# Loading the dense U columns by whole blocks into three buffers

## The chip, the cores and the metric

One core of a Trainium2 chip runs the whole kernel in one launch. The metric is device time in microseconds, the median of repeated runs. TensorE multiplies, VectorE and ScalarE split and copy, GpSimd issues row gathers, SyncE (SP) issues the plain loads. Each engine works through its own queue in order.

## The reference, cut to what matters

One residual block over T = 256 tokens of width D = 2048. Its last part is a retrieval layer over 16,384 = 128 x 128 experts. For every token and each of 8 heads the scores of two halves of a key choose 16 experts; with `emb_u` and `emb_v` (16,384 x 2048, f32):

```
u = emb_u[it];  a = einsum('td,thkd->thk', xt, u)
w = gelu(a) * gate
vv = emb_v[it]; y = einsum('thk,thkd->td', w, vv)
```

So for each token 128 rows of `emb_u` are dotted with the token's vector, and 128 rows of `emb_v` are summed with the weights that result.

## The kernel before

**The U stage.** The dots with `emb_u` are done in two ways at once. The first 768 of the 2048 columns (`UG`) are gathered: GpSimd fetches, for one of the 128 choices and 128 tokens, 128 rows of 768 columns (L757), and VectorE multiplies and sums them (L764). The other 1280 columns (`FK` = 10 slices of 128) are dense: all 16,384 experts are multiplied with all tokens on TensorE, and the wanted numbers are picked out later, from a table `A`. The dense part runs over 128 blocks of 128 experts, a block in two halves of 5 slices each: 256 half blocks, `n` = 0 to 255.

**One half block.** `u_load` (L702) loads 128 x 5 x 128 f32 (320 KB, 2560 contiguous bytes to a partition) into one of `UB` = 4 buffers `ub`. For n >= `DIRECT` = 34 it splits them so that TensorE can take them in its faster f32r format: ScalarE casts to `hi` (L711), VectorE subtracts, `lo = ub - hi` (L712), each into one of `UHB` = 3 buffers. `u_products` (L887) then makes 5 slices x 3 products: hi by both parts of the tokens' vectors, lo by the first. The half blocks below 34 are multiplied as they are, in f32 (`mmu<-x1T,ub`), straight out of `ub`. Four half blocks, two blocks of experts, share a PSUM bank; ScalarE copies it into `A` (L954).

**Order around it.** The first `FIRST` = 3 loads are issued before the routing jobs (L742). The room of `A` is free only when those jobs' tiles are, so the first finished bank is parked in a tile `set` (L907), which takes a buffer of the `ulo` tag, and is copied into `A` once the split operands 34 and 35 have been made (L956). 64 gathers are made early, during the routing; 16 are left for the stage after. The others are spread over the products at 0.733 a half block from n = 16 on: each waits for the products of its half block (L962), and its dot is put behind the lo split that was made last (L945), at most two gathers lying in flight before it (`BEHIND_U`). Gathers take four buffers: free `hT` tiles and one row tile.

The queues' orders are not written out by hand: a planner puts each instruction into its engine's queue by the time at which it expects the operands, so a load can stand before another that the program issues first. A buffer's load waits for the last reader of what lay there.

**After it.** The picking stage turns one-hot rows by a product with an identity in f32r, `idr`, which is cast on ScalarE in `columns()` (L873, called at n = `COLS`, but placed earlier by the planner). Then the V stage does the same with `emb_v`: dense columns as blocks of 736 KB (5888 contiguous bytes to a partition), split likewise, and gathered rows of 576 columns.

Of the kernel before, what the change touches and what calls it, by code (L numbers as in the profile page):

```python
# [10 lines left out]
F32 = mybir.dt.float32  # L11
F32R = mybir.dt.float32r
# [4 lines left out]
ALU = mybir.AluOpType  # L17
# [5 lines left out]
P = 128  # L23
T = 256
# [23 lines left out]
SC, QH = 3, 2  # L48
FIRST, DIRECT = 3, 34
EG, LG = 7, 2  # L50
UB, UHB = 4, 3
PRE, POOL, LEFT = 16, 0, 16
ADA_FROM, ADA_EVERY = 0, 3.4
LEAD, LAG, AHEAD1 = 1, 2, 1
# [6 lines left out]
FK = KD - UK  # L61
# [55 lines left out]
def block_kernel(ctx, tc, a, out):  # L117
    nc = tc.nc
    def pool(name, side, bufs=1, space=None):
        stack = ExitStack()  # L120
        kw = {} if space == bass.MemoryType.DRAM else {"reuse_waits": "tile"}
        if space is not None:
            kw["space"] = space
        return stack.enter_context(tc.tile_pool(name=name, bufs=bufs, side=side, **kw)), stack
# [5 lines left out]
    late = {}  # L130
# [9 lines left out]
    def bank(name):  # L140
        return late["side"].tile([P, 512], F32, tag="side", name=name)
# [5 lines left out]
    ident = kst[:, K_ID:K_ID + P]  # L147
# [159 lines left out]
    for j in range(D // GC + 1):  # L307
# [12 lines left out]
        if old is not None:  # L320
            hi, lo = loaded.pop(old)
# [376 lines left out]
    u_rows, u_cols, v_rows, v_cols = a["peer_u_rows"], a["peer_u_cols"], a["peer_v_rows"], a["peer_v_cols"]  # L698
    HALF = ((0, FK - FK // 2), (FK - FK // 2, FK))
    UH = FK - FK // 2  # L700

    def u_load(n):  # L702
        ub = late["p2"].tile([P, UH, P], F32, tag="ub", bufs=UB, name="ub")
        k0, k1 = HALF[n % 2]
        w = k1 - k0
        nc.sync.dma_start(ub[:, :w], u_cols[n // 2, :, k0:k1])
        if n < DIRECT:
            return ub, ub
        hi = late["p2"].tile([P, UH, P], F32R, tag="uhi", bufs=UHB, name="uhi")
        lo = late["p2"].tile([P, UH, P], F32R, tag="ulo", bufs=UHB, name="ulo")  # L710
        late["hi"] = nc.scalar.copy(hi[:, :w], ub[:, :w])  # L711
        late["lo"] = (nc.gpsimd if n < POOL else nc.vector).tensor_tensor(lo[:, :w], ub[:, :w], hi[:, :w].bitcast(F32), op=ALU.subtract)  # L712
        return hi, lo

    def norm2():
        drain()
        nc.sync.dma_start(ga2d, adaR[96:97])
        ssum = late["ssum"] = keep.tile([P, TT], F32, name="ssum")
        nc.vector.tensor_reduce(ssum, late["ss"], axis=AX.X, op=ALU.add)
        rsqrt(ssum, ssum, 1.0 / D)  # L720
        pr = bank("prs")
        for tt in range(TT):
            nc.tensor.matmul(pr[:, tt * P:(tt + 1) * P], ssum[:, tt:tt + 1].to_broadcast([P, P]), ident, start=True, stop=True)
        for c in range(KD // 2):
            v = late["x1T"][:, 2 * c:2 * c + 2]
            nc.vector.tensor_tensor(v, v, pr[:, None, :T].to_broadcast([P, 2, T]), op=ALU.mult)
            dst = h2T.add("h2T")
            for k in range(2):
                nc.scalar.activation(v[:, k], v[:, k], AF.Identity, bias=shc[:, 2 * c + k:2 * c + k + 1])
            put_split(dst, slice(0, 2), v)  # L730
        for c0 in range(0, UG, GC):
            psh = ada_bcast(1, c0, "psh2")
            for tt in range(TT):
                hr = h2b[:, tt, c0:c0 + GC]
                nc.vector.scalar_tensor_tensor(hr, hr, ssum[:, tt:tt + 1], psh, op0=ALU.mult, op1=ALU.add)
        sb_s.close()
        pg, late["pg_s"] = pool("pg", "left")
        late["pg"] = pg
        late["p2"], late["p2_s"] = pool("p2", "right")
        late["skT"] = pg.tile([P, 2 * HEADS, NK], F32, name="skT")  # L740
        nc.sync.dma_start(late["skT"], a["peer_subkeys"])
        late["u"] = [u_load(n) for n in range(FIRST)]  # L742
        late["pair"] = pg.tile([P, TT * 2, TOPK], F32, name="pair")
        nc.sync.dma_start(late["pair"].rearrange("p s a -> p (s a)"), a["const_index"][:, K_PAIR:])
# [125 lines left out]
        nc.vector.tensor_tensor(ex, ex, sm[:, :, :, None].to_broadcast([P, TT, HEADS, TOPK]), op=ALU.mult)  # L870

    def columns():
        nc.scalar.copy(idr, ident)  # L873
        for dst, src in ((i1T, i12[:, 0]), (i2T, i12[:, 1]), (gT, gate)):
            pt = bank("pt")
            for tt in range(TT):
                nc.tensor.transpose(pt[:, tt * P:(tt + 1) * P], src[:, tt], ident)
            nc.scalar.copy(dst, pt[:, :T])
            if dst is i2T:
                nc.scalar.mul(neg, pt[:, :T], -1.0)  # L880

    p2, p2_s = late["p2"], late["p2_s"]
# [4 lines left out]
    def u_products(n):  # L887
        for m in range(n + len(ready), min(n + (3 if n < DIRECT else 2), 2 * NK)):
            ready.append(u_load(m))
        hi, lo = ready.pop(0)  # L890
        first, last = n % 2 == 0, n % 2 == 1
        if n % 4 == 0:
            sums[n // 4] = bank("mmu").rearrange("p (b t) -> p b t", b=2) if n // 4 % 2 else pm.tile([P, 2, T], F32, tag="mm", name="mmu")
        acc = sums[n // 4][:, n // 2 % 2]
        k0, k1 = HALF[n % 2]
        steps = ((hi, 0), (hi, 1), (lo, 0)) if n >= DIRECT else ((hi, None),)
        for i, (w, part) in enumerate(steps):
            for k in range(k0, k1):
                x = late["x1T"][:, UK + k] if part is None else h2T.op(part, UK + k)
                mm = nc.tensor.matmul(acc, w[:, k - k0], x, start=(first and k == 0 and i == 0),  # L900
                                      stop=(last and k == FK - 1 and i == len(steps) - 1))
        return mm
# [1 line left out]
    staged = {}  # L904

    def stage(g):
        t = p2.tile([P, 2, T], F32, tag="ulo", bufs=UHB, name="set")  # L907
        nc.scalar.copy(t, sums.pop(g))
        staged[g] = t

    for n in range(DIRECT):
        mm = u_products(n)
        if n % 4 == 3 and not staged:
            stage(n // 4)
# [11 lines left out]
    pick_room, pick_room_s = pool("pickroom", "left")  # L926
    colT = pick_room.tile([P, 4, T], F32, name="colT")
    i1T, i2T, wT, gT = (colT[:, i] for i in range(4))
    neg = pick_room.tile([P, T], F32, name="neg")
    idr = pick_room.tile([P, P], F32R, name="idr")  # L930
    row_room, row_room_s = pool("rowroom", "left")
    flown, begun = [], 0

# [15 lines left out]
    for n in range(2 * NK):  # L949
        if n >= DIRECT:  # L950
            mm = u_products(n)
        if n % 4 == 3:
            src = staged.pop(n // 4) if n // 4 in staged else sums.pop(n // 4)
            put = nc.scalar.copy(A[:, n // 4], src.rearrange("p b (g s) -> p g b s", s=2))  # L954
            if n < DIRECT:
                tc.add_manual_dep(put.ins, split_ahead.ins.name, QUEUED, reason="the first split operands before the table")  # L956
        if n == COLS - 12:
            softmax(mm)
        if n == COLS:
            columns()  # L960
        while done < rate * (n + 1 - PRE):
            fly_u(*todo.pop(0), after=mm)  # L962
            done += 1
        while len(flown) > BEHIND_U:
            land_u()
# [10 lines left out]
    p2, p2_s = pool("pm2", "right")  # L976
# [4 lines left out]
        return b, b.rearrange("p (t n) -> p t n", t=4)  # L981

    agT = p2.tile([P, T], F32, name="agT")
    SET = 8
    iotas = iota[:, None, :].to_broadcast([P, SET, P])
    o1s, o2s = {}, {}

    def one_hot(q, u, on):
        t0 = u * SET
        o = p2.tile([P, SET, P], F32R if q else F32, tag=f"o{q}", bufs=O2 if q else O1, name="oh")  # L990
        ii = colT[:, q]
        cut = SET - (SHARE1 if u * SET < T // 2 else SHARE2)[q]
        if on == "V":
            nc.vector.tensor_tensor(o[:, :cut], iotas[:, :cut], ii[:, t0:t0 + cut, None].to_broadcast([P, cut, P]), op=ALU.is_equal)
        else:
            for t in range(cut):
                nc.scalar.activation(o[:, t], iota, AF.Square, bias=neg[:, t0 + t:t0 + t + 1])
            nc.scalar.activation(o[:, :cut], o[:, :cut].bitcast(F32), AF.Relu, bias=1.0, scale=-1.0)
        for t in range(cut, SET):
            nc.gpsimd.tensor_scalar(o[:, t], iota, ii[:, t0 + t:t0 + t + 1], None, op0=ALU.is_equal)  # L1000
        return o
# [3 lines left out]
    def turned(u):  # L1005
        for h in range(2):
            t0 = u * SET + 4 * h
            oh = p2.tile([P, 4, P], F32, tag="oh2T", bufs=OT, name="oh2T")
# [256 lines left out]
```

## Time and profile before

| | |
|---|---|
| median of 3 runs | 2291.24 us (2289.45 to 2292.52) |
| the profiled execution | 2295.83 us, its span 2294.0 us |
| TensorE busy | 2144.0 us, 93% |
| VectorE busy | 1784.8 us, 78% |
| ScalarE busy | 994.7 us, 43% |
| GpSimd busy | 941.0 us, 41% |
| DMA | 638.25 MB, mean 278 GB/s |
| granted TensorE clock, mean | 0.984 of full speed |

The span runs from the first to the last instruction of the profiled execution. Busy shares are averages over stages that have different limits. A row of the grouped view names line, engine, operation, output<-input, shape and count, then busy time and mean length, then the idle time of that engine just before these instructions and what ended it. PE is TensorE, PEld its weight loads, DVE is VectorE, ACT ScalarE, POOL GpSimd, SPq the queue of SP.

### The profile page before, as it was taken

The page shows a single profiled execution, that of the slowest core. Times are in us where ns is not written, and L with a number is a line of the kernel's source. Part 1 is how long each engine was busy: PE and PEld are TensorE (multiplying, and loading weights), DVE is VectorE, ACT ScalarE, POOL GpSimd, SP SyncE. Part 2 cuts the span into 40 slices and gives each one's busy share as a digit, 9 for nine tenths or more (in the row PEclk, how much of TensorE's full clock was granted, in tenths as well). Part 3 has the DMA queues.
Part 4 walks back from the last instruction along what each step waited for, and adds up shares of the span by engine and source line. Part 5 has one row for each costly group of instructions (what it writes and reads, how often), then busy time and mean ns, then how long its engine had stood idle before and what let it go on. Part 6 is the DMA issues. An engine that isn't in the chain of part 4 may idle for free. (4 is left out here: it accounts for less than half of the span.)

```text
span 2294.0 us, 37061 instructions
## 1 busy us (share of the span) xinstructions
PE 2144.0 (93%) x13886; PEld 1915.3 (83%) x13886; DVE 1784.8 (78%) x3400; ACT 994.7 (43%) x1424; POOL 941.0 (41%) x748
## 2 busy tenths in 40 slices
PE   6899999999999998999599999997889999999996
PEld 3578888999999977988589999997788887888885
DVE  3469888888888855688677777778997888888887
ACT  3235556553344445100244444446775434444443
POOL 0000000000000001566644444447996878878884
PEclk9999999999999999999899999998999999999998
DMA  9987787788878866668889999994205999999997
GB/s 356 371 308 267 285 284 278 276 291 291 298 281 292 310 212 216 220 221 282 284 303 324 324 317 314 306 325 138 62 2 179 335 325 327 327 337 328 334 328 269
DMA packets 144311, 638.25 MB, mean 278 GB/s; under 512 B 20721, under 2 KB 26625, under 8 KB 112001
## 3 DMA queue, kind: packets, MB, share of 16 engines
q1 hardware_dynamic: 102146, 459.65, 56.4%
q0 software_dynamic: 41984, 176.23, 22.6%
q8 instruction: 109, 1.79, 0.3%
q14 instruction: 72, 0.59, 0.1%
HBM read 631.59 MB, written 4.20 MB: 277 GB/s over the span
## 5 line engine op out<-in xcount | busy, mean ns | idle before, releaser
L757 POOL DMA_INDIRECT gat<-in_peer_v_rows,eidx x256 | 414.3, 1619 | 105.7 <-issue 40.9
L757 POOL DMA_INDIRECT gat<-in_peer_u_rows,eidx x256 | 316.0, 1234 | 284.9 <-PE mmu L900 190.4
L213 ACT CAST whi<-wt 128x2048 fp32r<-128x2048 f32 x128 | 244.4, 1909 | 274.7 <-PE mm L414 208.7
L764 DVE SCALAR_TENSOR_TENSOR gat<-gat,h2b 128x768 f32<-128x768 f32 x256 | 250.3, 980 | 117.4 <-DMA gat<-in_peer_u_rows,eidx 110.4
L215 DVE TENSOR_TENSOR wlo<-wt,whi 128x2048 fp32r<-128x2048 f32 (+1 forms) x128 | 289.3, 2260 | 53.0 <-ACT whi L213 49.4
L358 POOL DMA_DIRECT2D br<-in_b_ada x32 | 15.8, 495 | 763.8 <-DVE ada_acc L359 718.3
L900 PE MATMUL mmu<-h2T,uhi 128*128 128x256 f32 x2220 | 307.6, 286 | 11.4 <-ACT uhi L711 11.2
L1126 ACT CAST vh<-vb 128x1472 fp32r<-128x1472 f32 x128 | 183.1, 1430 | 299.2 <-DMA vb<-in_peer_v_cols 242.8
L711 ACT CAST uhi<-ub 128x640 fp32r<-128x640 f32 x222 | 161.3, 728 | 319.5 <-DMA ub<-in_peer_u_cols 265.7
L900 PEld LDWEIGHTS mmu<-h2T,uhi 128*128 128x128 f32 x2220 | 283.9, 193 | 17.0 <-ACT uhi L711 16.8
L1109 DVE SCALAR_TENSOR_TENSOR yg<-gat,wrow,yg 128x576 f32<-128x576 f32 x254 | 207.7, 818 | 73.2 <-DMA gat<-in_peer_v_rows,eidx 68.9
L355 DVE SCALAR_TENSOR_TENSOR ada_acc<-wa,sc_col,ada_acc 128x256 f32<-128x256 f32 x480 | 231.8, 483 | 11.5
L1128 DVE TENSOR_TENSOR vl<-vb,vh 128x1472 fp32r<-128x1472 f32 x128 | 215.7, 1685 | 12.6 <-ACT vh L1126 12.4
L1178 PE MATMUL yp<-vl,wh 128*128 128x512 f32 (+1 forms) x768 | 194.8, 387 | 11.5 <-DVE vl L1128 10.5
L900 PE MATMUL mmu<-h2T,ulo 128*128 128x256 f32 x1110 | 174.3, 288 | 32.8 <-DVE ulo L712 30.8
L1178 PE MATMUL yp<-vh,wh 128*128 128x512 f32 (+1 forms) x768 | 193.1, 385 | 4.5 <-ACT wh L1122 2.3
L712 DVE TENSOR_TENSOR ulo<-ub,uhi 128x640 fp32r<-128x640 f32 x222 | 180.1, 823 | 16.3 <-ACT uhi L711 12.4
L1178 PE MATMUL yp<-vh,wl 128*128 128x512 f32 (+1 forms) x768 | 192.1, 384 | 0.0
L900 PEld LDWEIGHTS mmu<-h2T,ulo 128*128 128x128 f32 x1110 | 150.1, 193 | 39.1 <-DVE ulo L712 34.9
L414 PE MATMUL mm<-whi,hT 128*128 128x512 f32 (+1 forms) x832 | 181.8, 363 | 0.0
L1178 PEld LDWEIGHTS yp<-vl,wh 128*128 128x128 f32 x768 | 142.1, 188 | 46.7 <-DVE vl L1128 20.6
L1178 PEld LDWEIGHTS yp<-vh,wh 128*128 128x128 f32 x768 | 144.9, 189 | 31.1 <-ACT vh L1126 3.5
(276 smaller groups left out, 3650.1 us busy)
## 6 DMA issues: line engine op xcount, KB each, us to landing
wa<-in_w_ada SPq DMA_DIRECT2D x96, 1024.0 KB
vb<-in_peer_v_cols SPq DMA_DIRECT2D x128, 736.0 KB
ub<-in_peer_u_cols SPq DMA_DIRECT2D x256, 320.0 KB
wt<-in_w_vg SPq DMA_DIRECT2D x32, 1024.0 KB
wt<-in_w_branch_gate SPq DMA_DIRECT2D x32, 1024.0 KB
wt<-in_w_u SPq DMA_DIRECT2D x16, 1024.0 KB
wt<-in_w_b_out SPq DMA_DIRECT2D x16, 1024.0 KB
wt<-in_w_o SPq DMA_DIRECT2D x16, 1024.0 KB
```

The lines of the kernel that those rows point to most:

```text
L213: nc.scalar.copy(hi, wt)
L215: nc.vector.tensor_tensor(lo[:, :cut], wt[:, :cut], hi[:, :cut].bitcast(F32), op=ALU.subtract)
L355: nc.vector.scalar_tensor_tensor(acc, wt[:, k], s, acc, op0=ALU.mult, op1=ALU.add)
L414: nc.tensor.matmul(job.ps[b], l, r, start=(first and k == 0 and i == 0 and not lo_part), stop=(last and k == job.rows - 1 and lo_part == 1))
L712: late["lo"] = (nc.gpsimd if n < POOL else nc.vector).tensor_tensor(lo[:, :w], ub[:, :w], hi[:, :w].bitcast(F32), op=ALU.subtract)
L757: d = nc.gpsimd.indirect_dma_start(out=g, out_offset=None, in_=table, in_offset=bass.IndirectOffsetOnAxis(ap=rows_of("idx")[:, tt, n:n + 1 ...
L764: return nc.vector.scalar_tensor_tensor(g, g, 1.0, h2b[:, tt, :UG], op0=ALU.mult, op1=ALU.mult, accum_out=pe["wrow"][:, tt, n:n + 1])
L900: mm = nc.tensor.matmul(acc, w[:, k - k0], x, start=(first and k == 0 and i == 0), stop=(last and k == FK - 1 and i == len(steps) - 1))
L1109: d = nc.vector.scalar_tensor_tensor(yg[:, tt], g, w, yg[:, tt], op0=ALU.mult, op1=ALU.add)
L1126: nc.scalar.copy(vh, vb)
L1128: late["split"] = nc.vector.tensor_tensor(vl, vb, vh.bitcast(F32), op=ALU.subtract)
L1178: return nc.tensor.matmul(yp[tt][n][:, :w], l[:, tt * P:(tt + 1) * P], r[:, c:c + w], start=(i == 0 and j == 0), stop=(i == NK - 1 and j = ...
```

## The change

Dense columns are loaded once a block (n even), all ten slices, 640 KB, 5120 contiguous bytes to a partition, into one of three buffers; the two halves are views of it. The split still goes by halves, into three hi buffers and two lo buffers in place of three. The parked bank takes a buffer of the hi tag. The f32r identity moves from the room that lasts through the U stage to that of the picking stage, and its cast from `columns()` to where that room is opened. In bytes of a partition: `ub` 10,240 to 15,360, lo 7680 to 5120.

```diff
-UB, UHB = 4, 3
+UB, UHB, ULB = 3, 3, 2
...
     def u_load(n):
-        ub = late["p2"].tile([P, UH, P], F32, tag="ub", bufs=UB, name="ub")
         k0, k1 = HALF[n % 2]
         w = k1 - k0
-        nc.sync.dma_start(ub[:, :w], u_cols[n // 2, :, k0:k1])
+        if n % 2 == 0:
+            late["ub"] = late["p2"].tile([P, FK, P], F32, tag="ub", bufs=UB, name="ub")
+            nc.sync.dma_start(late["ub"], u_cols[n // 2])
+        ub = late["ub"][:, k0:k1]
         if n < DIRECT:
             return ub, ub
         hi = late["p2"].tile([P, UH, P], F32R, tag="uhi", bufs=UHB, name="uhi")
-        lo = late["p2"].tile([P, UH, P], F32R, tag="ulo", bufs=UHB, name="ulo")
-        late["hi"] = nc.scalar.copy(hi[:, :w], ub[:, :w])
-        late["lo"] = (nc.gpsimd if n < POOL else nc.vector).tensor_tensor(lo[:, :w], ub[:, :w], hi[:, :w].bitcast(F32), op=ALU.subtract)
+        lo = late["p2"].tile([P, UH, P], F32R, tag="ulo", bufs=ULB, name="ulo")
+        late["hi"] = nc.scalar.copy(hi[:, :w], ub)
+        late["lo"] = nc.vector.tensor_tensor(lo[:, :w], ub, hi[:, :w].bitcast(F32), op=ALU.subtract)
         return hi, lo
...
     def columns():
-        nc.scalar.copy(idr, ident)
...
     def stage(g):
-        t = p2.tile([P, 2, T], F32, tag="ulo", bufs=UHB, name="set")
+        t = p2.tile([P, 2, T], F32, tag="uhi", bufs=UHB, name="set")
...
-    idr = pick_room.tile([P, P], F32R, name="idr")
...
     agT = p2.tile([P, T], F32, name="agT")
+    idr = p2.tile([P, P], F32R, name="idr")
+    nc.scalar.copy(idr, ident)
```

## Rows read from the trace of the kernel before

**Rows 1.** The page: busy us and instructions; DMA share and GB/s in 40 slices.

```profile
PE 2144.0 (93%) x13886; PEld 1915.3 (83%) x13886; DVE 1784.8 (78%) x3400; ACT 994.7 (43%) x1424; POOL 941.0 (41%) x748
...
DMA  9987787788878866668889999994205999999997
GB/s 356 371 308 267 285 284 278 276 291 291 298 281 292 310 212 216 220 221 282 284 303 324 324 317 314 306 325 138 62 2 179 335 325 327 327 337 328 334 328 269
```

**Rows 2.** Windows, U stage: length; busy us (count) by engine; clock, DMA share, GB/s.

```profile
1110.00:1150.00 40.00, 25.57 (x162) 23.86 (x163) 26.53 (x51) 13.68 (x23) 23.70 (x19) 0.84 0.87 285
1150.00:1550.00 400.00, 382.04 (x3083) 372.37 (x3082) 300.71 (x512) 173.87 (x262) 176.69 (x151) 1.00 0.94 317
```

**Rows 3.** Timeline of TensorE, 1096 to 1121: start, length, what, [idle before <-releaser].

```profile
1096.89 1.45 PE L900 MATMUL mmu<-h2T,uhi 128*128 128x256 f32 x10
1110.60 1.43 PE L900 MATMUL mmu<-h2T,ulo 128*128 128x256 f32 x5 [12.26 <-DVE ulo L712]
...
1116.59 1.47 PE L900 MATMUL mmu<-h2T,uhi 128*128 128x256 f32 x10 [1.36 <-ACT uhi L711]
```

**Rows 4.** Grouped instructions of 1150 to 1550 us.

```profile
L900 PE MATMUL mmu<-h2T,uhi 128*128 128x256 f32 x2052 | 282.1, 284 | 7.8 <-ACT uhi L711 7.8
L900 PEld LDWEIGHTS mmu<-h2T,uhi 128*128 128x128 f32 x2051 | 260.1, 191 | 12.4 <-ACT uhi L711 12.2
...
L712 DVE TENSOR_TENSOR ulo<-ub,uhi 128x640 fp32r<-128x640 f32 x206 | 167.1, 823 | 11.9 <-ACT uhi L711 8.3 <-PE mmu L900 1.4 <-issue 0.8
L900 PE MATMUL mmu<-h2T,ulo 128*128 128x256 f32 x1025 | 159.1, 286 | 10.1 <-DVE ulo L712 8.1 <-issue 1.3
L711 ACT CAST uhi<-ub 128x640 fp32r<-128x640 f32 x205 | 148.9, 728 | 227.9 <-DMA ub<-in_peer_u_cols 181.2 <-PE mmu L900 32.4 <-DVE ulo L712 9.3
...
L900 PEld LDWEIGHTS mmu<-h2T,ulo 128*128 128x128 f32 x1025 | 137.2, 191 | 15.2 <-DVE ulo L712 11.0 <-issue 4.0
```

**Rows 5.** Timeline of TensorE in the steady part, 1305 to 1316 us.

```profile
1307.45 0.76 PE L900 MATMUL mmu<-h2T,ulo 128*128 128x256 f32 x5
1308.05 1.36 PE L900 MATMUL mmu<-h2T,uhi 128*128 128x256 f32 x10
1309.25 0.76 PE L900 MATMUL mmu<-h2T,ulo 128*128 128x256 f32 x5
1309.85 1.36 PE L900 MATMUL mmu<-h2T,uhi 128*128 128x256 f32 x10
```

**Rows 6.** Waits, 1150 to 1550: us in total, times, longest.

```profile
DVE gat L764 <- DMA gat<-in_peer_u_rows,eidx: 84.8, 89, 4.0
```

**Rows 7.** Windows, the V stage.

```profile
1800.00:2250.00 450.00, 438.80 (x1961) 365.27 (x1960) 382.73 (x443) 190.69 (x217) 366.85 (x224) 1.00 0.94 330
```

**Rows 8.** Timeline of SP's queue, 1098 to 1112 us.

```profile
1110.57 1.76 SPq L706 DMA_DIRECT2D ub<-in_peer_u_cols  x4
```

**Rows 9.** Line 706 up to 1093.5: ns min/median/max, first and last start.

```profile
L706 SPq DMA_DIRECT2D ub<-in_peer_u_cols x36: 327/328/913, 904.7 to 1092.8; - x36
```

**Rows 10.** Waits of SP's queue, 1090 to 1125, then 1150 to 1550.

```profile
SPq L706 <- DVE ulo L712: 21.0, 4, 14.4
...
SPq L706 <- DVE ulo L712: 230.0, 164, 3.8
```

**Rows 11.** Timeline of ScalarE, then of VectorE, 1108 to 1122 us.

```profile
1110.59 3.51 ACT L954 COPY A<-mmu 128x512 f32<-128x512 f32 x7
1115.81 0.72 ACT L711 CAST uhi<-ub 128x640 fp32r<-128x640 f32 x1 [1.71 <-DMA ub<-in_peer_u_cols]
...
1116.57 0.83 DVE L712 TENSOR_TENSOR ulo<-ub,uhi 128x640 fp32r<-128x640 f32 x1 [3.53 <-ACT uhi L711]
```

**Rows 12.** Timeline of VectorE, 1305 to 1312 us.

```profile
1307.77 0.82 DVE L712 TENSOR_TENSOR ulo<-ub,uhi 128x640 fp32r<-128x640 f32 x1
...
1309.62 1.65 DVE L712 TENSOR_TENSOR ulo<-ub,uhi 128x640 fp32r<-128x640 f32 x2
```

**Rows 13.** Line 873, the identity's cast.

```profile
L873 ACT CAST idr<-kst x1: 302/302/302, 1032.1 to 1032.1; 128x128 fp32r<-128x128 f32 x1
```

## The prediction

> **What bounds the kernel now.** I read the page first [rows 1]: TensorE is busy 93% of the span, and the DMA engines stand at 9 tenths in the slices from 1204 to 1548 us, most of the U stage, which the change is about. No view of the whole span says which of the two binds there, so the stage was cut by time [rows 2].
>
> The U stage runs with split operands from 1097 us on, in three parts: a stop of 12.3 us [rows 3], a slow ramp from 1110 to 1150 with the granted clock at 0.84 of full speed, and 400 us of steady work with the clock at 1.00 (2.4 GHz), the DMA engines at 0.94 and 317 GB/s. In the steady part TensorE makes 2052 hi and 1025 lo matmuls [rows 4], 15 to a half block, so 205 half blocks at 1.95 us. Where nothing is waited for, a half block takes 1.80 us: first products at 1308.05 and at 1309.85 [rows 5]. So 205 x 1.80 = 369 us is TensorE's floor, and 31 us is all that any change to loads and buffers can win there.
>
> Who is late? By the grouped rows of this stretch [rows 4] TensorE stands idle 7.8 us before the hi products, for ScalarE, and 10.1 us before the lo products, 8.1 of it for VectorE; seen from the weight loads that go ahead of the products it is 12.4 and 15.2, nearly the whole 31. ScalarE in turn waits 181 us for dense columns to land; VectorE is busy 300.7 us and waits another 84.8 us, 89 times, for the row gathers [rows 2, 6]. So two streams are late about equally: dense columns by way of ScalarE, gathered rows by way of VectorE, both from the same DMA engines. TensorE is nearly full and so are they.
>
> **The change part by part.**
>
> *Whole blocks, three buffers.* Four buffers of half a block become three of a whole one: six halves of room for four. Now a half's buffer is refilled as soon as its own lo split is done, and used again four halves on (4 x 1.95 = 7.8 us, of which cast, 0.73, and split, 0.82, take their part). Afterwards the first half of a block is asked for when the split five halves before it ends, the second six: 9.8 and 11.7 us, while the larger load takes 655,360 B / 317 GB/s = 2.07 us of the engines where the smaller takes 1.03. So about 1 us more per load against 2 to 4 us more time. ScalarE's waits should mostly go, and with them TensorE's 7.8 us. What is late next is VectorE, whose gathers the change does not touch.
>
> Does the DMA side allow it? The stretch moves 317 GB/s x 400 us = 126.8 MB. The contiguous piece of one partition goes from 2560 B to 5120 B for the dense half of that traffic. The nearest stretch with larger pieces of both kinds (5888 B dense, gathers beside it) is the V stage, 330 GB/s at the same share 0.94 [rows 7]. At 330 the bytes take 384 us, 16 less; at 317, nothing is won. I take the middle, 8 us, which is also TensorE's wait for ScalarE. **Term: -8 us, bounds -31** (the floor) **and +23** (late gathers, the last rival below).
>
> The Trainium skill, "DMA: Bandwidth & Descriptors", Bandwidth, counts about 2 us fixed for each transfer on top of its bytes, and wants 1 MiB transfers. An estimate from that page's fit, 2.75 us for 320 KB and 3.5 us for 640 KB, would by itself bring the loads of the steady part from 564 to 359 us if they ran one at a time, and with that the whole 31 us. The trace doesn't bear the condition out: SP issues four of these loads within 1.76 us [rows 8], so whatever is fixed in them overlaps. Its result is the time of the first rival below.
>
> *The stop and the ramp.* In the 12.3 us stop TensorE waits for the first lo split [rows 3], which VectorE comes to only behind its dots with early gathered rows; the change touches neither, 0. But the ramp has a piece of its own: SP has issued 36 half loads by 1092.8 [rows 9] and then waits 14.4 us for a lo split [rows 10], though the room of halves 36 and 37 is that of 32 and 33, which TensorE reads directly and has left at 1096.89 [rows 3]. A load that waits for a split must stand before them in SP's order. They go out from 1110.57 on [rows 8], so ScalarE waits 1.71 us, VectorE 3.53 [rows 11] and TensorE 1.36 [rows 3]. With whole blocks the room for halves 36 and 37 is that of 30 and 31, free two direct halves sooner; that load should go before the stop and be there when ScalarE's copies end at 1114.1 [rows 11]. TensorE's wait makes 1.4 us, VectorE's 3.5 pulls the rest of the ramp in, part of which the gathers take back. **Term: -3 us.** Bounds: 0 if SP's order is as unlucky again; -13 if only VectorE's 26.5 us of work stayed of the ramp's 40 [rows 2].
>
> *Two lo buffers.* A lo split then waits for the product two halves before it, not three. It hardly ever would: the split at 1307.77 and the one at 1309.62 start with products before them long over, the second of them the one of 1307.45 [rows 5, 12]. Cover is lost only when VectorE would be over two halves ahead, and it finishes the split of 1307.77 at 1308.59, 0.66 us before its product at 1309.25. **Term: 0**, bounds 0 and +8.1, TensorE's waits on VectorE doubled. The staging copy moves from a lo to a hi buffer: freed by the first of ScalarE's table copies, which stand before the third cast in any case [rows 11]; 0, and at worst 0.73, a cast's length.
>
> *Half as many issues on SP.* 128 fewer at 0.33 us [rows 9] is 42 us of SP's queue, but in the steady part SP waits 230 us for splits [rows 10]: 0. Ahead of the stage three blocks go out in place of four halves: 0, at worst the 2.07 us that the two halves more take at 317 GB/s.
>
> *The identity copy.* One ScalarE cast of 302 ns at 1032 [rows 13] moves behind the U stage, because its room is freed only there, and holds up the first one-hots by its length. **Term: +0.3 us**, bounds 0 and 1.25: a gather still in its room costs 84.8 / 89 = 0.95 us on average.
>
> Sum: -8 - 3 + 0.3 = -10.7 us. The profiled execution took 2295.83 us (span 2294.0), which is 4.6 above the median of the runs; it would take 2285.1, and the median goes from 2291.24 to **2280.5 us**.
>
> **The rivals.**
>
> *The dense loads were all of it: faster by much.* If VectorE's lateness is itself a consequence of late casts, TensorE's floor is nearly reached: -26 of the 31 us and -5 of the ramp, 2260 us. For it: ScalarE's 181 us of waiting are by far the longest on a computing engine. Against: by its own rows VectorE waits only 8.3 us for casts, and 84.8 for gathers [rows 4, 6].
>
> *Nothing moves.* The DMA engines at 0.94 are full for the purpose, the size of the pieces changes little, and each byte earlier for a cast is a byte later for a gather; or SP's order holds the new loads as it held the old. -1, 2290 us. For it: 317 and 330 GB/s differ by 4% only.
>
> *Gathers crowded out: slower.* A gather that comes behind a dense load finds up to 1.03 us more in front of it, on average half, 0.52 us. On the 89 that are already waited for this is 46 us of VectorE. In-order, each late gather holds the next lo split. It decides from the point where the lateness passes VectorE's lead of some 0.7 us. If half of the 46 us reach TensorE, +23, against -8 and nothing else: +15, **2306 us**. For it: VectorE's 300.7 + 84.8 us and the 11.9 before its splits fill the stretch already. Against: gathers are issued as the products finish, so if products come sooner they do too. The Trainium skill's same page, Queues, rings and completion order, says that a DMA engine takes turns between its queues packet by packet; by that rule longer dense pieces give the gathers a smaller part of the engine, the direction of this rival. No row of before shows the turns themselves.
>
> **How the numbers follow.** Forecast (5 to 18 us faster) 0.42; much faster 0.20; nothing 0.16; slower 0.22. About 0.2%, 4.6 us, is what a measurement tells from no change: faster 0.62, same 0.16, slower 0.22. The range reaches down to 2262, the near side of the much-faster case (which leaves 0.08 below), and up to 2300, part of the way to the slow one (0.11 above). The likeliest case's own range is 2273 to 2286.
>
> **What would show it.** Right: in the steady part ScalarE's wait for the dense columns drops below 60 us, TensorE's wait for ScalarE below 3, the half block comes to 1.90 us or less at 325 GB/s or more, and the third cast follows ScalarE's copies without a wait. Wrong: VectorE's wait for gathers above 100 us with TensorE waiting on lo splits; or ScalarE still waiting as long, with GB/s unchanged; or a wait of VectorE for lo products, which would be the price of two buffers.

## The result: 1.7% slower, and the profile after

The changed kernel takes 2332.8 us (2319.93 to 2333.86, five runs) against 2291.24, where the forecast was 2280.5. The medians differ by 42 us; the ratio, taken over all runs of both and not from the two medians, is 1.0169, with a 95% interval of 1.0146 to 1.0191, which makes 39 us. Costs below are taken from ratios, except where medians are named. Line numbers are two or so higher than before (the cast is L713, the lo split L714, the products L901, the dot L766, the gather L759).

The span grew by 32.8 us, from 2294.0 to 2326.8. The last lo product of the U stage starts at 1598.4 us where it started at 1560.3, 38 us later, so all of the loss lies in that stage. The windows of the changed kernel (length; busy us and count by engine; clock, DMA share, GB/s) answer to [rows 2, 7]:

```profile
1110.00:1150.00 40.00, 28.87 (x177) 27.14 (x177) 26.70 (x52) 12.79 (x21) 21.63 (x19) 0.78 0.85 288
1150.00:1550.00 400.00, 354.88 (x2786) 344.05 (x2785) 266.21 (x463) 157.24 (x238) 156.67 (x136) 0.98 0.85 287
1840.00:2290.00 450.00, 443.62 (x1990) 370.91 (x1989) 388.27 (x449) 194.96 (x223) 359.79 (x227) 1.00 0.95 335
```

The ramp holds a few more matmuls (177 for 162). The steady part is the place: 2780 matmuls of the products, 185 half blocks, 2.16 us each in place of 1.95, which is 39 us over the 185. The DMA engines went from 0.94 to 0.85: they were not what held it back.

The grouped instructions of the same 400 us, to be read against [rows 4]; behind the second bar is the idle time before the group and who ended it:

```profile
L901 PE MATMUL mmu<-h2T,uhi 128*128 128x256 f32 x1853 | 257.0, 286 | 0.0
...
L901 PE MATMUL mmu<-h2T,ulo 128*128 128x256 f32 x927 | 149.9, 293 | 45.1 <-DVE ulo L714 44.9
L714 DVE TENSOR_TENSOR ulo<-ub,uhi 128x640 fp32r<-128x640 f32 x186 | 149.0, 820 | 9.2 <-issue 3.8 <-ACT uhi L713 2.8 <-PE mmu L901 2.6
L713 ACT CAST uhi<-ub 128x640 fp32r<-128x640 f32 x186 | 133.7, 727 | 242.4 <-DMA ub<-in_peer_u_cols 117.5 <-PE mmu L901 57.7 <-DVE ulo L714 56.6
L766 DVE SCALAR_TENSOR_TENSOR gat<-gat,h2b 128x768 f32<-128x768 f32 x136 | 130.1, 956 | 124.6 <-DMA gat<-in_peer_u_rows,eidx 124.2
```

In this stretch TensorE no longer waits for ScalarE at all (7.8 us before), but 44.9 us for VectorE's lo splits (8.1 before). VectorE's splits wait neither for casts (2.8) nor for a free lo buffer, that is for TensorE (2.6). What VectorE waits for is gathered rows: 124.2 us, against 84.8 in [rows 6], though there are fewer dots in the stretch.

One such stop, in the timelines of GpSimd, then VectorE, then TensorE (start, length, what, idle before and its releaser):

```profile
1370.83 1.38 POOL L759 DMA_INDIRECT gat<-in_peer_u_rows,eidx  x1 [2.54 <-PE mmu L901]
...
1374.93 0.82 DVE L714 TENSOR_TENSOR ulo<-ub,uhi 128x640 fp32r<-128x640 f32 x1
1379.09 0.96 DVE L766 SCALAR_TENSOR_TENSOR gat<-gat,h2b 128x768 f32<-128x768 f32 x1 [3.34 <-DMA gat<-in_peer_u_rows,eidx]
...
1379.98 1.55 DVE L714 TENSOR_TENSOR ulo<-ub,uhi 128x640 fp32r<-128x640 f32 x2
...
1376.50 1.36 PE L901 MATMUL mmu<-h2T,uhi 128*128 128x256 f32 x10
1380.85 1.44 PE L901 MATMUL mmu<-h2T,ulo 128*128 128x256 f32 x5 [2.99 <-DVE ulo L714]
```

The gather of 1370.83 is dotted at 1379.09 (both are the 164th of their kind; the products of half block 151 release it). VectorE stands 3.34 us before that dot, and behind it in the same queue is the lo split of half block 155 that TensorE needs; those of 152, 153 and 154 are ahead of it. TensorE stops for 2.99 us, and as gathers are issued behind products, the next gather comes later too.

So three splits, of the half blocks after the one that releases the gather, stand ahead of its dot. That count of splits was then taken from the queues' orders, for the 153 gathers that half blocks 41 to 249 release: **in the kernel before it is four for all 153; in the changed kernel four for 111 and three for 42.** The program's text asks for just that mixture: a dot comes two gathers after its own, and at 0.733 gathers a half block these are 2 or 3 half blocks; the split made last by then is that of the half block after, so 3 or 4 splits. In the kernel before, the planner had drawn one more split ahead of those 42 dots. Presumably it expected a lo buffer to be free by then, and with two buffers expects none; no run shows how the planner decides, only the orders that come of it. In the changed kernel the 42 dots stay where the program put them, one half block, 1.8 us, earlier.

How much time does a gather need? TensorE was ready for the lo products of half block 155 at 1380.85 - 2.99 = 1377.86, 7.0 us after the gather was issued. The dot (0.96) and the split (0.82) come before them, so the gather had some 5.2 us to land. Each further split ahead of a dot gives it a half block more, 1.80 us: 7.0 and 8.8 us. This is an estimate from one stop. The median gather from 1150 to 1500 us takes 6.0 us from issue to landing (count, then that median), and the one above 8.3:

```profile
gat<-in_peer_u_rows,eidx POOLq DMA_INDIRECT x119, 6.0
```

A stop also costs more than its length. In the one shown the granted clock, 1.00 from 1370 to 1378 us, is 0.76 from 1378 to 1385, part of it at 1.2 GHz in place of 2.4, and the five lo products behind the stop take 1.44 us where such a group takes 0.76 in [rows 5]:

```profile
1378.00:1385.00 7.00, 4.15 (x23) 4.15 (x24) 5.04 (x10) 2.01 (x3) 1.47 (x1) 0.76 0.57 172
```

Over the 400 us the clock is 0.98 in place of 1.00, by estimate up to 8 us (0.02 x 400) of what the 185 half blocks lose. TensorE's waits, seen from the weight loads as in the prediction, grew by more, from 27.6 to 56.0 us.

### The profile page after: what moved, and what is told of

Read it like the earlier page. It is cut to its first block, busy times and chain, and to the rows that moved or that the text cites. A ratio compares the mean times of both kernels' runs of the same rounds, so it can differ in the third digit from the quotient of the medians.

```text
span 2326.8 us, 36909 instructions
## 1 busy us (share of the span) xinstructions
PE 2152.3 (93%) x13886; PEld 1925.2 (83%) x13886; DVE 1779.4 (76%) x3400; ACT 993.1 (43%) x1424; POOL 923.4 (40%) x748
## 5 line engine op out<-in xcount | busy, mean ns | idle before, releaser
L759 POOL DMA_INDIRECT gat<-in_peer_v_rows,eidx x256 | 405.1, 1582 | 110.5 <-issue 34.1
L759 POOL DMA_INDIRECT gat<-in_peer_u_rows,eidx x256 | 307.4, 1201 | 328.6 <-PE mmu L901 235.9
L766 DVE SCALAR_TENSOR_TENSOR gat<-gat,h2b 128x768 f32<-128x768 f32 x256 | 250.3, 980 | 168.7 <-DMA gat<-in_peer_u_rows,eidx 168.1
L901 PE MATMUL mmu<-h2T,uhi 128*128 128x256 f32 x2220 | 310.7, 288 | 0.6 <-ACT uhi L713 0.6
L713 ACT CAST uhi<-ub 128x640 fp32r<-128x640 f32 x222 | 159.5, 728 | 355.4 <-DMA ub<-in_peer_u_cols 206.0
L901 PEld LDWEIGHTS mmu<-h2T,uhi 128*128 128x128 f32 x2220 | 290.8, 197 | 0.8 <-ACT uhi L713 0.8
L901 PE MATMUL mmu<-h2T,ulo 128*128 128x256 f32 x1110 | 181.7, 296 | 68.8 <-DVE ulo L714 68.6
L901 PEld LDWEIGHTS mmu<-h2T,ulo 128*128 128x128 f32 x1110 | 153.0, 197 | 82.6 <-DVE ulo L714 82.3
L714 DVE TENSOR_TENSOR ulo<-ub,uhi 128x640 fp32r<-128x640 f32 x222 | 177.9, 820 | 10.3 <-ACT uhi L713 3.9
```

Source lines behind the costliest of these rows:

```text
L714: late["lo"] = nc.vector.tensor_tensor(lo[:, :w], ub, hi[:, :w].bitcast(F32), op=ALU.subtract)
L759: d = nc.gpsimd.indirect_dma_start(out=g, out_offset=None, in_=table, in_offset=bass.IndirectOffsetOnAxis(ap=rows_of("idx")[:, tt, n:n + 1 ...
L766: return nc.vector.scalar_tensor_tensor(g, g, 1.0, h2b[:, tt, :UG], op0=ALU.mult, op1=ALU.mult, accum_out=pe["wrow"][:, tt, n:n + 1])
```

## The experiments

The theory formed from this, the order theory: a gather with three splits' time is often late, and VectorE, in order, passes the lateness on. The rival, from the prediction, is crowding: 640 KB loads keep the gathers back. A third possibility is that two lo buffers cost by being few, whatever the order. Each run was timed beside the kernel before on the same chip, the first four runs below on one chip and the last four on another; all ratios are to that kernel.

**Two lo buffers alone.** The kernel before, half-block loads and all, with

```diff
-UB, UHB = 4, 3
+UB, UHB, ULB = 4, 3, 2
-        lo = late["p2"].tile([P, UH, P], F32R, tag="ulo", bufs=UHB, name="ulo")
+        lo = late["p2"].tile([P, UH, P], F32R, tag="ulo", bufs=ULB, name="ulo")
-        t = p2.tile([P, 2, T], F32, tag="ulo", bufs=UHB, name="set")
+        t = p2.tile([P, 2, T], F32, tag="uhi", bufs=UHB, name="set")
```

> The kernel before with its half-block loads and four half buffers, and only the lo buffers cut from three to two (the parked bank in a hi buffer). In VectorE's queue this puts 42 of the 153 dots of the steady U stage one lo split earlier behind their gather (three splits between in place of four), as in the changed kernel. Order theory (a gather has one half block less time before VectorE stands still for it): 2320 to 2335 us, VectorE's wait for gathers in 1150 to 1550 us about 120 us (84.8 before, 124.2 changed), TensorE's wait for lo splits about 45. Crowding theory (640 KB loads keep the gathers back): 2285 to 2297, waits as before.

Measured 2325.9 us, ratio 1.0162 (1.0114 to 1.0209). No load was changed, and the whole loss is there. The order of dots and splits is the changed kernel's from the first to the last. VectorE's wait for gathers, 113.5 us, came a little under what was expected, and TensorE's for lo splits, 34.4, a quarter under.

**The order alone.** The kernel before, three lo buffers and all, with each split pinned behind the dot that the program makes before it:

```diff
+        if "dot" in late:
+            tc.add_manual_dep(late["lo"].ins, late["dot"].ins.name, QUEUED, reason="behind the dot before it")
         return hi, lo
...
-        d = times(*flown.pop(0))
+        d = late["dot"] = times(*flown.pop(0))
```

> The kernel before with three lo buffers and half-block loads, nothing changed but VectorE's order: every lo split is put behind the dot that the program makes before it, which gives the changed kernel's order of dots and splits exactly. Order theory: 2320 to 2335 us, as the changed kernel. Crowding theory: 2285 to 2297. If the room of two lo buffers itself costs, and not the order: 2285 to 2297 too, with the run of two lo buffers slow.

Measured 2329.35 us, ratio 1.0178 (1.013 to 1.0225). The third lo buffer is there, and does not help: it is the place in the queue that costs, not the room. (The order is the changed kernel's for all 153 gathers, four splits for 111 and three for 42; only among the first ten splits, in the ramp, does it differ. ScalarE's order of casts and copies is the same in all the kernels of this document.) The grouped rows of 1150 to 1550 us show the same picture as the changed kernel's:

```profile
L902 PE MATMUL mmu<-h2T,ulo 128*128 128x256 f32 x950 | 152.6, 292 | 34.8 <-DVE ulo L712 33.7
...
L766 DVE SCALAR_TENSOR_TENSOR gat<-gat,h2b 128x768 f32<-128x768 f32 x140 | 134.0, 957 | 120.9 <-DMA gat<-in_peer_u_rows,eidx 120.7
```

**The changed kernel with its dots put back.** `at` is the half block that releases the gather; its dot comes three half blocks later, which places all 153 behind the fourth split:

```diff
-        flown.append((g, tt, n))
+        flown.append((g, tt, n, at))
...
-        while len(flown) > BEHIND_U:
+        while flown and flown[0][3] <= n - 3:
             land_u()
```

> The changed kernel (640 KB loads, two lo buffers) with the dots placed as in the kernel before: each stands behind the fourth lo split after its gather was issued, for all 153. Order theory: 2265 to 2292 us, the gain that was forecast or at least the time before; VectorE's wait for gathers at or under 85 us in the steady part. Crowding theory: 2315 or more. If two lo buffers cost by room: 2310 or more, with VectorE waiting for TensorE's lo products.

Measured 2299.38 us, ratio 1.0039 (1.0019 to 1.0059). Of the ratio's 0.0169 of loss 0.0130 is undone, some 30 of 39 us, but it missed the range: the kernel is still slower than before, by some 9 us. So there is a second, smaller cost, and no gain from the whole blocks. TensorE still waits 28.1 us for lo splits, and VectorE 106.9 for gathers.

**Half loads into whole-block buffers.** The changed kernel, with

```diff
-            nc.sync.dma_start(late["ub"], u_cols[n // 2])
         ub = late["ub"][:, k0:k1]
+        nc.sync.dma_start(ub, u_cols[n // 2, :, k0:k1])
```

> The changed kernel with its three whole-block buffers and two lo buffers, each block fetched by two loads of 320 KB (2560 B to a partition) in place of one of 640 KB. Order theory: 2318 to 2337 us, no better than the changed kernel. Crowding theory: 2285 to 2300, since the loads are those of before.

Measured 2320.96 us, ratio 1.0131 (1.0083 to 1.0179): still slow, as the order theory has it. It may be better than the changed kernel, but the two intervals overlap.

**Half loads and the dots put back.** Both edits together, to see the size of a load with the order held:

> Three whole-block buffers and two lo buffers, each block fetched by two loads of 320 KB, and every dot behind the fourth lo split after its gather: only the size of a load differs from the run of the changed kernel with dots placed as before (2299 us). If 640 KB loads cost by holding gathers back (the 8 us left there): 2283 to 2294 us, VectorE's wait for gathers back to some 85 us in 1150 to 1550. If the 8 us come from two lo buffers or from the whole-block buffers: 2296 to 2303.

Measured 2291.65 us, ratio 1.0003 (0.9991 to 1.0016), against 1.0039 with 640 KB loads. The intervals don't meet (the two runs are of different chips, each against the kernel before on its own): the load's size costs 0.0036, some 8 us, where the gathers have four splits' time. That is the crowding rival, true but small, and the traces show it: a gather lands a little later beside 640 KB loads. The rows are the changed kernel with its dots put back, then this run, 1150 to 1500 us (count, median us from issue to landing):

```profile
gat<-in_peer_u_rows,eidx POOLq DMA_INDIRECT x129, 6.4
gat<-in_peer_u_rows,eidx POOLq DMA_INDIRECT x133, 6.2
```

In the other two pairs it is 6.0 against 5.7 (3 or 4 splits) and 6.8 against 6.6 (five, below). It is not by way of ScalarE: VectorE's splits wait 1.1 us for casts with 640 KB loads and 0.4 with half loads, and TensorE 28.1 and 15.7 us for lo splits. VectorE's wait for gathers did not come back to 85: it is 99.8. And three buffers of whole blocks, together with two lo buffers, win nothing by themselves.

**Five splits, in the kernel before.** The same edit with `n - 4` in place of `n - 3`, and nothing else:

> The kernel before with one edit: every dot stands behind the fifth lo split after its gather, not the fourth. If a gather's time between issue and dot is what binds the U stage (order theory, in the other direction): faster, 2270 to 2286 us, VectorE's wait for gathers well below 84.8 us. If the dense columns bind once gathers have four splits: 2288 to 2296, no change.

Measured 2271.01 us, ratio 0.9912 (0.9893 to 0.9931). The lever works in the other direction too, with loads and buffers untouched. The window of 1150 to 1500 us, and VectorE's wait for gathers (total, times, longest) from 1150 to 1550, where the U stage now ends at 1532:

```profile
1150.00:1500.00 350.00, 346.86 (x2873) 345.00 (x2872) 281.47 (x477) 163.07 (x245) 159.81 (x141) 1.00 0.96 338
DVE gat L764 <- DMA gat<-in_peer_u_rows,eidx: 24.8, 39, 1.7
```

A half block takes 1.83 us. VectorE's splits now wait for casts (48.6), so here dense columns are next.

**Five splits, in the changed kernel**, again `n - 4`:

> The changed kernel, every dot behind the fifth lo split. Order theory: faster than with four (2299), 2268 to 2290 us, and by the theory that 640 KB loads hold gathers back for about half a load, that lateness is now covered. If the time lost is not the gathers': 2296 or more.

Measured 2270.76 us, ratio 0.9902 (0.9879 to 0.9924). With five splits' time the 640 KB loads no longer cost anything that these runs can tell.

**Five splits, whole-block buffers, half loads:**

> Three whole-block buffers, two lo buffers, 320 KB loads, every dot behind the fifth lo split. If both the place of the dots and the size of the loads count: the fastest of all, 2262 to 2284 us, with TensorE at 1.83 to 1.90 us a half block. If the DMA engines are full as they are: no better than the kernel before with five splits.

Measured 2266.91 us, ratio 0.9891 (0.9871 to 0.9912), 24 us below the kernel before by the medians, where the changed kernel was 42 above. It has the lowest median, though its interval overlaps the two runs above. Its steady part is at TensorE's floor, as the window of 1150 to 1520 us and the grouped rows of 1150 to 1526 show:

```profile
1150.00:1520.00 370.00, 369.97 (x3082) 369.58 (x3081) 298.05 (x512) 175.29 (x263) 200.87 (x152) 1.00 0.96 342
```

```profile
L901 PE MATMUL mmu<-h2T,uhi 128*128 128x256 f32 x2083 | 284.1, 283 | 0.0
...
L901 PE MATMUL mmu<-h2T,ulo 128*128 128x256 f32 x1043 | 159.4, 283 | 0.0
...
L766 DVE SCALAR_TENSOR_TENSOR gat<-gat,h2b 128x768 f32<-128x768 f32 x154 | 147.3, 957 | 54.4 <-DMA gat<-in_peer_u_rows,eidx 53.2
```

TensorE waits for nobody. 3082 matmuls in 370 us are 1.80 us a half block, better than the 1.83 to 1.90 expected. VectorE still waits 53.2 us for gathers, and it costs nothing, since the splits behind are early enough.

The runs as one table (time ratio to the kernel before; "splits" is the count told above):

| ub buffers | load | lo buffers | splits | ratio |
|---|---|---|---|---|
| 4 halves | 320 KB | 3 | 4 | 1 (the kernel before) |
| 4 halves | 320 KB | 2 | 3 or 4 | 1.0162 |
| 4 halves | 320 KB | 3 | 3 or 4 | 1.0178 |
| 3 blocks | 320 KB | 2 | 3 or 4 | 1.0131 |
| 3 blocks | 640 KB | 2 | 3 or 4 | 1.0169 (the changed kernel) |
| 3 blocks | 640 KB | 2 | 4 | 1.0039 |
| 3 blocks | 320 KB | 2 | 4 | 1.0003 |
| 4 halves | 320 KB | 3 | 5 | 0.9912 |
| 3 blocks | 640 KB | 2 | 5 | 0.9902 |
| 3 blocks | 320 KB | 2 | 5 | 0.9891 |

The ratio goes with the column of splits, and hardly with any other.

## Why the prediction was wrong

*Two lo buffers, term 0: this step failed.* It priced a wait for a free buffer, and that wait is indeed next to nothing (2.6 us after, 1.4 before). But the number of buffers also decides where the planner puts a split among the dots. The term alone, two lo buffers with all else as before, measures 0.0162 of 2291.86 us, 37 us, where its upper bound was 8.1; the same order with three lo buffers measures 0.0178. The step cited the splits at 1307.77 and 1309.62 [rows 12] for a wait, and did not ask what stands between them, and why.

*Whole blocks, three buffers, term -8.* The mechanism was half right, and its worth was not. TensorE's wait for ScalarE went from 7.8 to 0, as forecast. ScalarE's own wait for dense columns fell only from 181.2 to 117.5 us, not below 60, in part because ScalarE now waits for others; with the dots put back it is 168.6. The other stream, of which the prediction said itself that it was late about equally, then bound alone: with four splits for every gather, the term measures 0 with half loads and +9 us with whole ones. Taking TensorE's wait for one stream as what relieving it gives back does not hold when both must arrive for each half block. The 2 us a transfer that the prediction weighed and set aside stand in the Trainium skill ("DMA: Bandwidth & Descriptors") under "Anatomy of one DMA", as a fit for transfers that GpSimd issues; SP issues these loads, and no run here shows a fixed cost.

*The DMA engines are "nearly full": wrong.* The step took 0.94 for a limit and weighed 317 against 330 GB/s. With five splits the kernel before, its loads and buffers untouched, moves 338 GB/s at 0.96, and the run with whole-block buffers and half loads 342 at 0.96, with the same pieces of 2560 B. The engines' share followed the wait; it did not set it.

*The floor of 1.80 us a half block* held, and the last of the experiments reaches it.

*The ramp, term -3.* Right in its mechanism; its size is not shown. The third cast now follows ScalarE's copies with the data there, where [rows 11] had it wait until 1115.81; timeline of ScalarE:

```profile
1109.11 3.51 ACT L954 COPY A<-mmu 128x512 f32<-128x512 f32 x7
1112.44 0.79 ACT L713 CAST uhi<-ub 128x640 fp32r<-128x640 f32 x1
```

The ramp's window holds 15 matmuls more, one half block, some 1.8 us at the floor's pace. But from trace to trace this count varies by more: 160 and 192 in the runs of the order alone and of two lo buffers alone, which load as before, 150 to 199 with whole-block buffers. SP still waits 12.8 us for a split there, for a later block.

*The identity, +0.3.* The cast takes 301 ns at 1599.2, behind the last products, and the first product with it starts 4.4 us after the last lo product where it was 4.1 before, as forecast.

```profile
L985 ACT CAST idr<-kst x1: 301/301/301, 1599.2 to 1599.2; 128x128 fp32r<-128x128 f32 x1
```

*The slow rival* named the right engines, and its sign in the profile came true: VectorE's wait for gathers above 100 us, TensorE waiting on lo splits. But its cause, the size of a load, explains some 8 us of the 39, and the median gather is 0.2 to 0.3 us later, where 0.52 on average was estimated. The same rows had two causes, and only the runs that changed one of them told them apart. The Trainium skill ("DMA: Bandwidth & Descriptors", Queues, rings and completion order), by which a DMA engine takes turns between its queues, fits the direction of those 8 us; no run here shows the turns.

Left open: the span grew by 5 us less than the U stage, so later stages gave something back. The V stage's window has 335 GB/s in place of 330. No run was made on this, and the kernel before itself ranged from 2281.78 to 2302.86 us on one of the chips.

## What to carry to other kernels

A buffer count is also an input of whatever orders the queues: before pricing a buffer as room, compare the order of the instructions on each in-order engine, count what stands between a load's issue and the instruction that waits for it, and hold that time against the time that the load takes to land. Where two streams feed one engine, relieving one may give nothing until the other has slack; here one half block more of time for the gathers was worth more than any change of buffers that was tried. A DMA share near 0.94 is not a proof of a limit; see whether the rate rises when a wait is taken away.

## What was not expected of the hardware

With loads and buffers untouched, the mixed stream of dense loads and row gathers went from 317 to 338 GB/s, and the DMA engines' share from 0.94 to 0.96, by placing VectorE's dots one split later. Loads of twice the size, with pieces of 5120 B to a partition in place of 2560, were no faster in the mixed stream: the kernel takes 1.0039 against 1.0003 with four splits, and the two are not to be told apart with five.
